# Fourteen stores moved to ScalarE's queue, a third modulation buffer, and other request points in the feed-forward sections of a two-block network

## The chip, the cores and the metric

One core of a Trainium2 chip runs the whole network for one sequence of 256 tokens. The metric is device time in microseconds from launch to end. Names of engines in views: PE is TensorE (PEld its weight loads), DVE is VectorE, ACT is ScalarE, POOL is GpSimd, SP is SyncE, which issues nearly all DMAs here.

## The reference, cut to what matters

Two blocks of two layers each run one after the other on a [256, 1024] activation, in float32. A layer of the first block is a feed-forward section, a mixer, and a second feed-forward section; each is modulated by vectors that are made from `c`:

```
mod = (silu(c) @ ada_w[l] + ada_b[l]).reshape(1, 3, 3, 1, 1024)   # 9 vectors a layer
u = modulate(h, mod[0, 0], mod[0, 1])                             # h * (1 + scale) + shift
y = (silu(u @ w_gate) * (u @ w_up)) @ w_down                      # 1024 -> 2816 -> 1024
h = layer_norm(alpha * h + 0.5 * mod[0, 2] * y, g, b)
... mixer (convolution, state-space and attention branches), layer_norm, then the same again
```

A layer of the second block is a mixer of attention and mLSTM, and a feed-forward section `x + relu(rms(x) @ w_ff1)**2 @ w_ff2` (1024 to 4096 to 1024); it has no modulation.

## The kernel before

**Weights.** Each weight is packed in halves of 128x1024 float32 (512 KB). One half is one `Unit`. `load_half` (L181) issues its DMA from SyncE into the ring `raw` (4 buffers), ScalarE copies it to `hi` in the fast float format (L187), VectorE makes the rest `lo = raw - hi` (L188), and TensorE multiplies three times, hi by hi, lo by hi, hi by lo (L284 to L286 where weights are the stationary side, L297 to L299 where they are the moving side). `run` keeps at most LIVE = 4 split units ahead of the one being multiplied.

**A feed-forward section** of the first block has 11 column chunks. Chunk j gives four units for the hidden layer (gate and up, L284 to L286), then the two `down` units of chunk j-1, so six units in a round (four in the second block). The product of gate and up, `t2d` (L808), is made on VectorE, and its split `q` on ScalarE (L701) and VectorE (L702) feeds `down`. The last four `down` units are held back and run as `row_tail`: first the upper 128 tokens, then `stats(0)`, then the lower 128 tokens. I call the sections A (layer 0, first), B (layer 0, second), C (layer 1, first), D (layer 1, second), and E and F in the second block. A has 50 units after its hand-written start, B, C and D 66.

**A boundary** (`Ln`) needs rows of gains: `fetch` loads `grow` (the gate row, through DRAM) and two `lnrow` rows, 512 KB each. `stats` (L608, L609) multiplies and adds them and takes mean and variance of each row; `nb` (L615) then lets ScalarE normalise (L619) and TensorE transpose (L432). `early` splits the first four units of the next section into spare buffers; `prefetch` ends both.

**Sides.** Work beside the units is a generator in `sides`; after each unit `step_sides` advances it by its rate. `ada_stream` makes the modulation vectors: 128 tiles of 512 KB, each loaded by SyncE (L491) into the ring `ada` and multiplied and summed on VectorE (L492). A section sets its pace with `set_pace`, whose first tile has to stay behind `src.ins`, the last instructions of the operand of that section.

**Order.** The program text gives an order; a scheduler at build time then gives each engine its own list, by what it thinks to be ready and which buffers are free. Every engine runs its list strictly from front to back, SyncE's DMA issues too: an issue that waits for its buffer holds all issues behind it.

Of the kernel before, what the change touches and what calls it, by code (L numbers as in the profile page):

```python
# [19 lines left out]
P = 128  # L20
T = 256
D = 1024
# [83 lines left out]
def net_kernel(ctx, tc, a, out, dbg=None):  # L106
# [382 lines left out]
    def ada_tile(l, j, k, col, raw):  # L489
        n = D  # L490
        nc.sync.dma_start(raw, a["adaw"][l, j, k // 2][:, (k % 2) * n:(k % 2 + 1) * n])  # L491
        V.scalar_tensor_tensor(raw, raw, 1.0, crow, op0=ALU.mult, op1=ALU.mult, accum_out=col[:, k:k + 1])  # L492
# [4 lines left out]
    def ada_stream():  # L497
        for l, j in [(l, j) for l in range(DEPTH) for j in range(9)][2:]:
            col = const.tile([P, KT], F32, name="mod%d_%d" % (l, j))
            for k in range(KT):  # L500
                with behind(pace["after"]):
                    ada_tile(l, j, k, col, rt("ada", D, 2))
                pace["after"] = ()
                yield
            V.tensor_add(col, col, adb[:, l, j * 8:j * 8 + 8])
            mods[(l, j)] = col
            if j % 3 == 2:
                yield
                tp = tp_tile()
                E.transpose(tp[0:KT, :P], col, ident)  # L510
                gr = rt("t1", T, 4)[0:KT, :P]
                S.activation(gr, tp[0:KT, :P], AF.Copy, scale=(1.0 if j == 5 else 0.5))
                nc.sync.dma_start(growd[l * 3 + j // 3].rearrange("(k p) -> k p", p=P), gr)
                mods[(l, j, "row")] = True

    def set_pace(r, after=None):
# [33 lines left out]
            late_load(rows[tt], hd[tt])  # L550
            yield

    def start_fetch(nx):

        state["fetch"] = add_side(nx.fetch(), 1.0)

    def early(nx, n=4, rate=1.0):

# [6 lines left out]
    class Ln:  # L565
# [60 lines left out]
        def residual(self, tts=(0, 1)):  # L626
            with behind(self.ins):
                for tt in tts:
                    r = self.rows[tt]
                    V.tensor_mul(r, r, self.gr[0])  # L630
                    V.tensor_add(r, r, self.gr[1])
                    S.activation(r, r, AF.Copy, scale=ALPHA)
                    if self.i == 0:
                        nc.sync.dma_start(hd[tt], r)
            if 1 in tts:
                dump("h%d%d" % (self.l, self.i), self.rows)

    class Rms:
# [30 lines left out]
        def residual(self):  # L669
            if self.src:  # L670
                for tt in range(2):
                    nc.sync.dma_start(hd[tt], self.rows[tt])

    def rms_norm(row, pre, eps, out, sq, prepare=None):

# [85 lines left out]
    def ffn(cols, down, nj, src, act, rows, nxt):  # L761

        xT = lambda: src.xT
        y, hids, items = {}, {}, []

        def hidden(j):
            st = []

            def evac(ps):
                r = act(st, ps)  # L770
                if r is not None:
                    hids[j] = split_hidden(r)
            its = []
            for c in cols(j):
                its += proj_cols(c, xT, evac)
            return its
        hold = {"nx": nxt(y)}
        n0 = NFIRST if isinstance(src, First) else 2 // len(cols(0))
        done = 0
        for j in range(n0 - 1, nj):  # L780
            if j >= n0:
                items += hidden(j)
            elif isinstance(src, First):
                first = sum((cols(i) for i in range(n0)), [])
                items.append(lambda: src.start(first, rows, hids))
                continue
            else:
                items += first_hidden(sum((cols(i) for i in range(n0)), []), xT, rows, lambda: None, hids)
            if j == n0 + 1:
                items.append(src.residual)  # L790
            items += sum(down_items(y, hids, down, nj, range(done, j), hold), [])
            done = j
            if j == nj - 3:
                items.append(lambda: start_fetch(hold["nx"]))
            if j == nj - 4:
                items.append(lambda: early(hold["nx"], 4, 1.0))
            if j == nj - 2:
                items.append(lambda: hold["nx"].prefetch())
        items += sum(down_items(y, hids, down, nj, [nj - 1], hold), [])
        return items, hold["nx"]  # L800
# [1062 lines left out]
    def ffn_section(cols, down, nj, act, rows, nxt, tiles):  # L1863
        src = cur
        items, nx = ffn(cols, down, nj, src, act, rows, nxt)
        src.pre += set_early(items)
        us = [i for i, it in enumerate(items) if isinstance(it, Unit)]
        rate = tiles / (len(us) - 7)
        if isinstance(src, First):
            items.insert(us[1], lambda: set_pace(rate, src.ins))  # L1870
            items.insert(us[1], lambda: src.finish())
        elif rate:
            items.insert(us[3], lambda: set_pace(rate, src.ins))
        return items, nx
# [41 lines left out]
    class Bridge(Rms):  # L1916
# [12 lines left out]
        def start(self):  # L1929
            self.rows = self.ln.rows  # L1930
            for tt in range(2):
# [2 lines left out]
                    self.ln.stats(1)  # L1934
                self.norm[tt] = rms_norm(self.rows[tt], 1.0, 1e-6, self.n[tt], self.n[tt], self.prepare(tt))
                self.operand(tt)
                nc.sync.dma_start(hd[tt], self.rows[tt])
                if tt == 0:
                    state["after"] = self.ins
            dump("h12", self.rows)  # L1940
# [234 lines left out]
```

## Time and profile before

| | us |
|---|---|
| median of 3 runs | 2551.43 (2548.42 to 2554.11) |
| the profiled execution, its own time | 2554.82 |
| span in its profile | 2552.7 |

The profile counts the span from the first to the last instruction of the program; 2.1 us lie around it. TensorE is the busy engine. Its matmuls overlap, so its busy time says less than its waits: a wait of TensorE names the instruction that waited and what it waited for.

### The profile page before, as it was taken

How to read it: one execution, taken by the hardware profiler on the slowest of the kernel's cores; microseconds unless marked ns; L12 is line 12 of the kernel's file. 1: busy time of each engine (PE TensorE's matmuls, PEld its weight loads, DVE VectorE, ACT ScalarE, POOL GpSimd, SP SyncE). 2: the span in 40 equal slices, each digit the busy share in tenths (PEclk: the TensorE clock that was granted, in tenths of full speed). 3: DMA queues.
4: the chain of work that ended last, by engine and by line, in shares of the span. 5: the costliest groups of instructions: out<-in, count | busy, mean ns of one | idle time of the engine just before them, and what ended most of it. 6: DMA issues, size and time to landing. Idle time of an engine off the chain costs nothing.

```text
span 2552.7 us, 42530 instructions
## 1 busy us (share of the span) xinstructions
PE 2438.5 (96%) x16604; PEld 2208.8 (87%) x16604; DVE 1839.7 (72%) x3270; ACT 1344.2 (53%) x2356; POOL 69.8 (3%) x128
## 2 busy tenths in 40 slices
PE   8999999989889989989999999999899999999999
PEld 6887889889878879978898999899789898789888
DVE  7768988899786676768988996655766555656554
ACT  5444666544543444435666546545465555555554
POOL 0000000000000000000000000000100000100000
PEclk9999999999999999989999999999999999999999
DMA  9886622256868868875522357457335456436454
GB/s 332 286 301 226 217 101 92 91 171 216 270 218 279 272 205 275 273 242 173 166 67 84 117 188 231 143 189 250 119 121 185 156 187 223 134 100 223 141 187 143
DMA packets 134218, 484.73 MB, mean 190 GB/s; under 512 B 15569, under 2 KB 16129, under 8 KB 134018
## 3 DMA queue, kind: packets, MB, share of 16 engines
q1 hardware_dynamic: 133442, 480.83, 57.0%
q8 instruction: 130, 2.13, 0.3%
q10 hardware_dynamic: 576, 1.19, 0.1%
q14 instruction: 70, 0.57, 0.1%
HBM read 476.69 MB, written 5.27 MB: 189 GB/s over the span
## 4 chain that ended last, share of the span: by engine, by line
PE 61%; DMA 15%; DVE 13%; ACT 5%; issue 4%; POOL 1%; SPq 0%; ACTq 0%; DVEq 0%; POOLq 0%
PE mm L284 10%; PE mm L285 10%; PE mm L286 10%; DMA ada<-in_adaw_dram 8%; PE y L297 6%; PE y L298 6%; PE y L299 6%; DVE lo L188 4%; DVE ca L1204 2%; PE tp L989 2%; ACT hi L187 2%; DMA raw<-in_wg_dram 2%; DVE ada L492 1%; PE tp L980 1%; DMA raw<-in_wo_dram 1%
## 5 line engine op out<-in xcount | busy, mean ns | idle before, releaser
L187 ACT ACTIVATE hi<-raw 128x1024 fp32r<-128x1024 f32 (+1 forms) x676 | 712.6, 1058 | 725.1 <-PE mm L285 367.2
L188 DVE TENSOR_TENSOR lo<-raw,hi 128x1024 fp32r<-128x1024 f32 (+1 forms) x676 | 822.2, 1221 | 304.7 <-ACT hi L187 300.9
L284 PE MATMUL mm<-xTh,hi 128*128 128x256 f32 x2896 | 827.8, 286 | 10.3 <-ACT av L1222 3.0
L286 PE MATMUL mm<-xTh,lo 128*128 128x256 f32 x2896 | 824.2, 285 | 6.5 <-DVE lo L188 6.5
L285 PE MATMUL mm<-xTl,hi 128*128 128x256 f32 x2896 | 822.5, 284 | 2.4 <-DVE xTl L455 2.4
L284 PEld LDWEIGHTS mm<-xTh,hi 128*128 128x128 f32 x2896 | 551.2, 190 | 15.9 <-ACT av L1222 3.7
L286 PEld LDWEIGHTS mm<-xTh,lo 128*128 128x128 f32 x2896 | 550.8, 190 | 9.6 <-DVE lo L188 9.0
L285 PEld LDWEIGHTS mm<-xTl,hi 128*128 128x128 f32 x2896 | 550.7, 190 | 6.5 <-DVE xTl L455 3.2
L299 PE MATMUL y<-hi,q 128*128 128x512 f32 x664 | 264.5, 399 | 1.0 <-DVE q L702 1.0
L492 DVE SCALAR_TENSOR_TENSOR ada<-ada,crow 128x1024 f32<-128x1024 f32 x128 | 156.1, 1221 | 120.7 <-DMA ada<-in_adaw_dram 120.5
L297 PE MATMUL y<-hi,q 128*128 128x512 f32 x552 | 221.8, 402 | 14.2 <-ACT q L701 14.2
L298 PE MATMUL y<-lo,q 128*128 128x512 f32 x552 | 220.7, 400 | 5.0 <-DVE lo L188 5.0
L1204 DVE SCALAR_TENSOR_TENSOR ca<-av,pcol,ca 128x244 f32<-128x244 f32 (+26 forms) x480 | 207.3, 461 | 0.3
L299 PEld LDWEIGHTS y<-hi,q 128*128 128x128 f32 x664 | 126.4, 190 | 32.4 <-DVE q L702 2.0
L297 PEld LDWEIGHTS y<-hi,q 128*128 128x128 f32 x552 | 105.3, 191 | 39.0 <-ACT q L701 16.6
L298 PEld LDWEIGHTS y<-lo,q 128*128 128x128 f32 x552 | 104.9, 190 | 29.5 <-DVE lo L188 7.5
L297 PE MATMUL y<-hi,xTh 128*128 128x512 f32 (+1 forms) x288 | 114.1, 396 | 3.1 <-DVE e8b L830 1.5
L284 PE MATMUL mm<-xyh,hi 128*128 128x256 f32 x384 | 112.2, 293 | 4.2 <-ACT t2d L1366 4.2
L285 PE MATMUL mm<-xyl,hi 128*128 128x256 f32 x384 | 111.7, 291 | 4.4 <-DVE xyl L415 4.4
L286 PE MATMUL mm<-xyh,lo 128*128 128x256 f32 x384 | 111.1, 290 | 0.8 <-DVE lo L188 0.8
L299 PE MATMUL y<-hi,xTl 128*128 128x512 f32 (+1 forms) x288 | 111.1, 386 | 0.0
L298 PE MATMUL y<-lo,xTh 128*128 128x512 f32 (+1 forms) x288 | 110.7, 384 | 0.0
(492 smaller groups left out, 3730.5 us busy)
## 6 DMA issues: line engine op xcount, KB each, us to landing
ada<-in_adaw_dram SPq DMA_DIRECT2D x128, 512.0 KB, 5.2
raw<-in_ff_dram SPq DMA_DIRECT2D x128, 512.0 KB, 4.6
raw<-in_wg_dram SPq DMA_DIRECT2D x88, 512.0 KB, 5.6
raw<-in_wu_dram SPq DMA_DIRECT2D x88, 512.0 KB, 5.6
raw<-in_wd_dram SPq DMA_DIRECT2D x88, 512.0 KB, 5.4
raw<-in_wG_dram SPq DMA_DIRECT2D x48, 512.0 KB, 4.2
raw<-in_wkv_dram SPq DMA_DIRECT2D x16, 512.0 KB, 4.6
raw<-in_wval_dram SPq DMA_DIRECT2D x16, 512.0 KB, 4.3
```

What stands on the lines that cost most here:

```text
L187: S.activation(hi, raw, AF.Copy)
L188: eng.tensor_tensor(lo, raw, f(hi), op=ALU.subtract)
L284: E.matmul(ps, wh[:, wk + k], xh, start=(k == 0), stop=False)
L285: E.matmul(ps, wh[:, wk + k], xl, start=False, stop=False)
L286: E.matmul(ps, wl[:, wk + k], xh, start=False, stop=(k == nk - 1))
L297: return [E.matmul(ps, xh, wh[:, kk, cs], start=first, stop=False), E.matmul(ps, xh, wl[:, kk, cs], start=False, stop=False), E.matmul(ps, ...
L298: E.matmul(ps, xh, wl[:, kk, cs], start=False, stop=False),
L299: E.matmul(ps, xl, wh[:, kk, cs], start=False, stop=last)]
L492: V.scalar_tensor_tensor(raw, raw, 1.0, crow, op0=ALU.mult, op1=ALU.mult, accum_out=col[:, k:k + 1])
L980: E.transpose(tp[:, tsl(r * nbr + b)], pr[:, r, b, tsl(kt)], ident)
L989: E.matmul(o[:, i * HD:(i + 1) * HD], pTs[kt][:, tsl(i)], vof(i % nbr, kt), start=(kt == 0), stop=(kt == tt))
L1204: V.scalar_tensor_tensor(ca[:, k, s:T], av[:, 0:T - s], caw[:, k, w:w + 1], ca[:, k, s:T], op0=ALU.mult, op1=ALU.add)
```

## The change

Four things change. The ring `ada` gets a third buffer. Fourteen stores that depend on computed rows (eight of `hd`, six of `growd`) are issued by ScalarE in place of SyncE. In feed-forward sections `fetch` is asked for 32 units' worth of rounds ahead of the last chunk at 0.2 steps a unit (before: two chunks ahead, one step a unit), `early` 24 units ahead at 0.25 (before: three chunks ahead, one a unit), and `prefetch` after the last hidden chunk (before: one chunk sooner). The pace of `ada_stream` in a feed-forward section goes from 26/(units - 7) to 26/(units - 18) steps a unit: 0.60 to 0.81 in A, 0.44 to 0.54 in B, C and D.

```
--- before.py
+++ after.py
@@ ada_stream
                 with behind(pace["after"]):
-                    ada_tile(l, j, k, col, rt("ada", D, 2))
+                    ada_tile(l, j, k, col, rt("ada", D, 3))
                 pace["after"] = ()
...
                 S.activation(gr, tp[0:KT, :P], AF.Copy, scale=(1.0 if j == 5 else 0.5))
-                nc.sync.dma_start(growd[l * 3 + j // 3].rearrange("(k p) -> k p", p=P), gr)
+                S.dma_start(growd[l * 3 + j // 3].rearrange("(k p) -> k p", p=P), gr)
@@ start_fetch
-    def start_fetch(nx):
+    def start_fetch(nx, rate=1.0):
 
-        state["fetch"] = add_side(nx.fetch(), 1.0)
+        state["fetch"] = add_side(nx.fetch(), rate)
@@ Ln.residual
                     S.activation(r, r, AF.Copy, scale=ALPHA)
                     if self.i == 0:
-                        nc.sync.dma_start(hd[tt], r)
+                        S.dma_start(hd[tt], r)
@@ Rms.residual
                 for tt in range(2):
-                    nc.sync.dma_start(hd[tt], self.rows[tt])
+                    S.dma_start(hd[tt], self.rows[tt])
@@ ffn
             done = j
-            if j == nj - 3:
-                items.append(lambda: start_fetch(hold["nx"]))
-            if j == nj - 4:
-                items.append(lambda: early(hold["nx"], 4, 1.0))
-            if j == nj - 2:
+            per = 2 * len(cols(0)) + 2
+            if j == nj - 1 - 32 // per:
+                items.append(lambda: start_fetch(hold["nx"], 0.2))
+            if j == nj - 1 - 24 // per:
+                items.append(lambda: early(hold["nx"], 4, 0.25))
+            if j == nj - 1:
                 items.append(lambda: hold["nx"].prefetch())
@@ ffn_section
-        rate = tiles / (len(us) - 7)
+        rate = tiles / (len(us) - 18)
@@ Bridge.start
                 self.operand(tt)
-                nc.sync.dma_start(hd[tt], self.rows[tt])
+                S.dma_start(hd[tt], self.rows[tt])
```

What the scheduler makes of it is seen in the lists of the engines. Numbers in names are buffers of one tile each; the `mod` name says which vector the product goes to.

**The first tile of a pace.** SyncE's list in the middle of section B, before, from the load of the tile whose product must stay behind C's operand (`ada_9902`):

```order
L491 DMA ada_9902<-in_adaw_dram 128x1024
L181 DMA raw_8531<-in_wu_dram 128x1024
L491 DMA ada_9968<-in_adaw_dram 128x1024
L181 DMA raw_8552<-in_wu_dram 128x1024
L181 DMA raw_8583<-in_wd_dram 128x1024
L491 DMA ada_10043<-in_adaw_dram 128x1024
L181 DMA raw_8618<-in_wd_dram 128x1024
L181 DMA raw_8649<-in_wg_dram 128x1024
```

VectorE's list at the start of C, before, where that tile is used:

```order
L188 TENSOR_TENSOR lo_9759<-raw_9756,hi_9758 128x1024
L455 TENSOR_TENSOR xTl_9669<-t2_9732,xTh_9668 128x2x128
L455 TENSOR_TENSOR xTl_9669<-t2_9737,xTh_9668 128x2x128
L814 TENSOR_TENSOR t2d_9811<-t2d_9811,mm_9762 128x256
L492 SCALAR_TENSOR_TENSOR ada_9902,mod1_2_9294<-ada_9902,crow_95 128x1024
L759 TENSOR_TENSOR q4_9814<-tp_9815,q4_9814 128x2x128
L505 TENSOR_TENSOR mod1_2_9294<-mod1_2_9294,adb_86 128x8
```

18 products of other tiles stand between that load and this use, so the tile keeps one of the two `ada` buffers from the middle of B to the start of C.

SyncE's list in section B with the change, from the load of the corresponding tile (`ada_9871`):

```order
L491 DMA ada_9871<-in_adaw_dram 128x1024
L181 DMA raw_8592<-in_wu_dram 128x1024
L491 DMA ada_9988<-in_adaw_dram 128x1024
L181 DMA raw_8623<-in_wd_dram 128x1024
L491 DMA ada_10056<-in_adaw_dram 128x1024
L181 DMA raw_8658<-in_wd_dram 128x1024
L491 DMA ada_10097<-in_adaw_dram 128x1024
L181 DMA raw_8689<-in_wg_dram 128x1024
```

VectorE's list at the start of C with the change, where it is used:

```order
L815 TENSOR_TENSOR t2d_9862<-t2d_9862,mm_9813 128x256
L455 TENSOR_TENSOR xTl_9720<-t2_9783,xTh_9719 128x2x128
L455 TENSOR_TENSOR xTl_9720<-t2_9788,xTh_9719 128x2x128
L492 SCALAR_TENSOR_TENSOR ada_9871,mod1_4_9488<-ada_9871,crow_95 128x1024
L759 TENSOR_TENSOR q4_9865<-tp_9866,q4_9865 128x2x128
L505 TENSOR_TENSOR mod1_4_9488<-mod1_4_9488,adb_86 128x8
```

The tile is kept over the end of B as before, now as one of three buffers, and its load stands later (the 93rd tile in SyncE's list, before the 79th).

**End of C.** VectorE's list before, from the next to last `k` split to the first boundary row (`t2d` is the last hidden product, `q` its split, `y` the first row product of the boundary):

```order
L702 TENSOR_TENSOR q_11419<-t2d,q_11419 128x512
L188 TENSOR_TENSOR lo<-raw,hi 128x1024
L188 TENSOR_TENSOR k_11470<-raw,zc 128x1024
L492 SCALAR_TENSOR_TENSOR ada,mod_8_16208<-ada,crow 128x1024
L188 TENSOR_TENSOR lo<-raw,hi 128x1024 x2
L492 SCALAR_TENSOR_TENSOR ada,mod_8_16208<-ada,crow 128x1024
L188 TENSOR_TENSOR lo<-raw,hi 128x1024 x2
L492 SCALAR_TENSOR_TENSOR ada,mod_8_16208<-ada,crow 128x1024
L808 TENSOR_TENSOR t2d<-t2d,mm 128x512
L188 TENSOR_TENSOR lo<-raw,hi 128x1024
L702 TENSOR_TENSOR q_11595<-t2d,q_11595 128x512
```

The same place with the change:

```order
L702 TENSOR_TENSOR q_11480<-t2d,q_11480 128x512
L188 TENSOR_TENSOR lo<-raw,hi 128x1024
L188 TENSOR_TENSOR k_11539<-raw,zc 128x1024
L188 TENSOR_TENSOR lo<-raw,hi 128x1024 x4
L809 TENSOR_TENSOR t2d<-t2d,mm 128x512
L188 TENSOR_TENSOR lo<-raw,hi 128x1024
L702 TENSOR_TENSOR q_11666<-t2d,q_11666 128x512
```

The three `ada` products are gone from this place; the splits `lo` stay. In SyncE's list the last of all 128 `ada` loads stands ahead of C's `grow` row now; before, six of them stood behind it.

**End of B.** VectorE's list before, from the first row product of the boundary to `nb`:

```order
L608 TENSOR_TENSOR y_7991<-y_7991,grow 128x512
L608 TENSOR_TENSOR row_7219<-row_7219,y_7991 128x512
L609 BN_STATS bnst<-row_7219 128x6
L492 SCALAR_TENSOR_TENSOR ada,mod_4_10704<-ada,crow 128x1024
L608 TENSOR_TENSOR y_7991<-y_7991,grow 128x512
L608 TENSOR_TENSOR row_7219<-row_7219,y_7991 128x512
L609 BN_STATS bnst<-row_7219 128x6
L465 BN_AGGR bnmv<-bnst 128x2
L460 TENSOR_SCALAR rstd<-bnmv 128x1
L615 SCALAR_TENSOR_TENSOR nb<-bnmv,rstd 128x1
```

The same place with the change:

```order
L608 TENSOR_TENSOR y_8025<-y_8025,grow 128x512
L492 SCALAR_TENSOR_TENSOR ada,mod_7_11142<-ada,crow 128x1024
L608 TENSOR_TENSOR row_7250<-row_7250,y_8025 128x512
L609 BN_STATS bnst<-row_7250 128x6
L608 TENSOR_TENSOR y_8025<-y_8025,grow 128x512
L492 SCALAR_TENSOR_TENSOR ada,mod_7_11142<-ada,crow 128x1024
L608 TENSOR_TENSOR row_7250<-row_7250,y_8025 128x512
L492 SCALAR_TENSOR_TENSOR ada,mod_7_11142<-ada,crow 128x1024
L609 BN_STATS bnst<-row_7250 128x6
L465 BN_AGGR bnmv<-bnst 128x2
L460 TENSOR_SCALAR rstd<-bnmv 128x1
L615 SCALAR_TENSOR_TENSOR nb<-bnmv,rstd 128x1
```

One `ada` product stood between the first row product and `nb`; three stand there now.

In numbers over SyncE's list: the `ada` loads ahead of the next section's first `wval` load are 34 in A (before 26), and 24 units from A's `grow` row to the last `down` load are accompanied by 18 `ada` loads, 4 early units and 3 rows (in the last 24 units before: 10, 4 and 3).

## Rows read from the trace of the kernel before

**Rows 1.** The page, part 1: busy us, share, instructions.

```profile
PE 2438.5 (96%) x16604; PEld 2208.8 (87%) x16604; DVE 1839.7 (72%) x3270; ACT 1344.2 (53%) x2356; POOL 69.8 (3%) x128
```

**Rows 2.** Windows: length, then busy us (instructions) PE, PEld, DVE, ACT, POOL; clock; DMA.

```profile
73.00:221.00 148.00, 139.93 (x897) 125.72 (x897) 103.10 (x136) 58.56 (x65) 0.55 (x1) 0.99 0.84 290
720.00:934.00 214.00, 198.44 (x1343) 180.11 (x1341) 151.14 (x207) 93.04 (x120) 1.12 (x2) 0.98 0.77 257
934.00:1143.00 209.00, 197.64 (x1337) 181.99 (x1337) 146.65 (x202) 89.72 (x113) 1.14 (x2) 0.97 0.76 255
1608.00:1804.00 196.00, 191.40 (x1337) 178.22 (x1337) 116.74 (x134) 91.95 (x118) 2.00 (x3) 0.99 0.57 189
```

**Rows 3.** Waits in section A (73:221): total us, times, longest.

```profile
DVE ada L492 <- DMA ada<-in_adaw_dram: 25.0, 19, 2.7
...
PE y L297 <- ACT q L701: 3.3, 1, 3.3
```

**Rows 4.** Waits in section B (720:934).

```profile
DVE ada L492 <- DMA ada<-in_adaw_dram: 44.9, 25, 4.1
...
PE y L297 <- ACT q L701: 4.6, 1, 4.6
...
PE mm L286 <- DVE lo L188: 3.0, 5, 1.1
...
PE y L298 <- DVE lo L188: 2.6, 4, 1.1
```

**Rows 5.** Waits in section C (934:1143).

```profile
DVE ada L492 <- DMA ada<-in_adaw_dram: 43.9, 22, 3.7
...
PE y L297 <- ACT q L701: 5.3, 1, 5.3
...
PE mm L284 <- ACT hi L187: 1.9, 1, 1.9
```

**Rows 6.** Waits in section D (1608:1804).

```profile
PE tp L432 <- ACT t L452: 1.2, 1, 1.2
```

**Rows 7.** Windows at the ends of B and C (columns as in Rows 2).

```profile
917.20:927.40 10.20, 8.29 (x19) 6.03 (x20) 6.33 (x10) 0.63 (x1) 0.00 (x0) 0.50 0.64 224
1091.30:1098.00 6.70, 6.09 (x28) 6.09 (x29) 5.88 (x7) 4.06 (x5) 0.00 (x0) 0.50 0.78 244
1128.80:1135.60 6.80, 5.05 (x12) 3.99 (x13) 3.57 (x7) 0.63 (x1) 0.00 (x0) 0.50 0.66 244
```

**Rows 8.** VectorE in order of time, end of C (1114:1131.5).

```profile
1123.00 1.23 DVE L492 SCALAR_TENSOR_TENSOR ada<-ada,crow 128x1024 f32<-128x1024 f32 x1 [3.69 <-DMA ada<-in_adaw_dram]
...
1129.15 0.68 DVE L808 TENSOR_TENSOR t2d<-t2d,mm 128x512 f32<-128x512 f32 x1
```

**Rows 9.** VectorE in order of time, middle of B (800:815).

```profile
807.66 1.23 DVE L492 SCALAR_TENSOR_TENSOR ada<-ada,crow 128x1024 f32<-128x1024 f32 x1 [3.43 <-DMA ada<-in_adaw_dram]
```

**Rows 10.** SyncE in order of time, middle of B (800:815).

```profile
808.92 0.33 SPq L491 DMA_DIRECT2D ada<-in_adaw_dram  x1
```

**Rows 11.** Windows: the first 50 us, and the last 69 us of A.

```profile
0.00:50.00 50.00, 38.38 (x146) 29.08 (x147) 36.94 (x60) 22.60 (x27) 0.20 (x4) 1.00 0.96 359
142.00:211.00 69.00, 60.93 (x418) 55.36 (x418) 49.78 (x60) 31.48 (x34) 0.00 (x0) 1.00 0.88 302
```

**Rows 12.** DMA issues: KB each, median us to landing.

```profile
raw<-in_wg_dram SPq DMA_DIRECT2D x88, 512.0 KB, 5.6
...
t<-in_lnrow_dram SPq DMA_DIRECT2D x12, 512.0 KB, 8.3
```

**Rows 13.** SyncE's own waits, whole span.

```profile
SPq L491 <- DVE ada L492: 230.1, 81, 7.9
...
SPq L634 <- ACT row L632: 16.9, 4, 5.1
```

**Rows 14.** The page, part 5: split of a weight half on ScalarE and VectorE (busy, mean ns).

```profile
L187 ACT ACTIVATE hi<-raw 128x1024 fp32r<-128x1024 f32 (+1 forms) x676 | 712.6, 1058 | 725.1 <-PE mm L285 367.2
L188 DVE TENSOR_TENSOR lo<-raw,hi 128x1024 fp32r<-128x1024 f32 (+1 forms) x676 | 822.2, 1221 | 304.7 <-ACT hi L187 300.9
```

## The prediction

> **What bounds the kernel now.** I began with the page's first part: TensorE is busy for 96% of the span [rows 1], so time can only be won where it stands still or runs at a lower clock. The second view was windows by section. B, C and D have the same 66 units and nearly the same TensorE instructions (1343, 1337, 1337), yet take 214, 209 and 196 us [rows 2]. D is the yardstick: it fetches rows and early units at the same points as B and C, but has no `ada` stream; its DMA share is 0.57 against 0.77 and 0.76, its clock 0.99 against 0.98 and 0.97. So B holds 18 us and C 13 us that D doesn't have. D's 196/66 = 2.97 us is the price of a unit, and A's 148/50 = 2.96 us says that A holds almost nothing to win.
>
> The third view was waits by section, to see what fills those 18 and 13 us. In B TensorE waits 4.6 us in one piece for `q`, and 3.0 and 2.6 us in nine short ones for `lo` [rows 4]; in C 5.3 us for `q` and 1.9 us for `hi` [rows 5]; D's largest wait is 1.2 us and there is none for `q` [rows 6]. To that comes a lower clock: three stretches at 0.50, which is 1.2 of 2.4 GHz, 10.2 us at B's end and 6.7 and 6.8 us at C's [rows 7]. In the stretches at the ends TensorE had stood in those waits or in the boundary just before. At half clock the same matmuls take twice as long, so such a stretch costs at most half its length.
>
> The fourth view says why `q` is late. VectorE works its list from front to back, and in it `ada` products wait for their own loads: 44.9 us in B, 43.9 us in C, 25.0 us in A [rows 3 to 5]. At C's end one product starts at 1123.00 after 3.69 us of such a wait, and the last hidden product `t2d`, from which `q` is split, only runs at 1129.15 [rows 8]. The loads are late because only one of the two `ada` buffers turns round: the other one keeps the first tile of the next pace, which must stay behind the next operand. In the middle of B the product ends at 807.66 + 1.23 = 808.89 [rows 9], and SyncE issues the next load at 808.92 [rows 10]. Over the span SyncE was held so 81 times, 230.1 us in all, 2.84 us each [rows 13].
>
> **The change, part by part.** The sum is made against the profiled execution, 2554.82 us; this is 3.4 us above the median of 2551.43, so 3.4 comes off at the end.
>
> *Third buffer and higher pace, section C.* Two buffers turn round, and the stream has ended ahead of C's `grow` row. The three products in front of the last `t2d` are gone, and with them the waits that `q` stood behind. To win: 5.3 + 1.9 us of waits and half of 6.7 + 6.8 us, 13.9 us in all. The boundary of a section without `ada` still shows D's 1.2 us, and some of the low clock may be due to the boundary itself, so I take 11. Two products of 1.23 us also leave the row chain of the boundary, where TensorE stands still: 2.4 more, as they are ahead of `nb` there. Together **-13**, which is also C's whole distance from D. Bounds: -4 if only one of waits and clock goes partly, -17 if everything goes.
>
> *Section B.* To win: 4.6 + 3.0 + 2.6 us of waits and half of 10.2 us, 15.3 us. The tile for C's operand is still parked, but two buffers are left, not one; `ada` products go on to B's end, so I take two thirds, -10. Against it, three products stand in the row chain ahead of `nb`, before one: 2 x 1.23 = +2.4. Sum **-8**. Bounds: -15, and +5 if the waits stay and the chain's products have to wait for a load as that of 807.66 did (3.43 us).
>
> *Section A.* Here 8 more `ada` tiles than before fall in the section. From the `grow` row on, 24 units go with 18 `ada` loads, 4 early units and 3 rows: 49 loads of 512 KB, 25.7 MB. The time for 24 units is 24 x 2.97 = 71.3 us, so 360 GB/s are asked for. The last 69 us of A gave 302 GB/s at a DMA share of 0.88 [rows 11], which is 343 GB/s if it were full: 74.9 us, 3.6 us short. The four live units can hide some of that, and A's 3.3 us for `q` may go or stay; I take **+3**. Bounds: 25.7 MB at the 302 GB/s as delivered are 85 us, +14; if the shortage is hidden and the `q` wait goes, -3. VectorE has room: 49.78 of 69 us busy now, 8 more products of 1.23 us make it 59.6 us, 86%. A rule of the Trainium skill bears on this term ("DMA: Bandwidth & Descriptors", section "Bandwidth", Where 436 GB/s comes from): between HBM and SBUF the memory's side limits a core to about 358 GB/s. By it the 25.7 MB take an estimated 71.8 us, the live units hide the rest, the term would be 0 and the sum 3 us lower. The first 50 us of this trace show 359 GB/s at a share of 0.96, which agrees with that figure; the stretch in A doesn't reach it.
>
> *`fetch`, `early`, `prefetch` at other points.* The same 3 rows and 4 units are loaded, spread over more units. No wait for a row stands among the waits of A to D, and a row lands 8.3 us after its issue, under three units [rows 12]. In D, E and F this is the only part of the change besides stores; D has 1.2 us to give. I take **-1** for the three together (0 to -2). `prefetch` moves by one chunk, and what it waits for was landed long before. The early splits are the same work, 1.06 us on ScalarE and 1.22 us on VectorE for a unit [rows 14].
>
> *Fourteen stores by ScalarE.* SyncE was held 16.9 us in four waits for the rows that it stored [rows 13], with weight loads behind them. No wait for weights of that size shows in TensorE, since units are loaded ahead, so nothing is won that isn't counted above. On ScalarE an issue costs about the 0.33 us of SyncE's [rows 10], 14 x 0.33 = 4.6 us on an engine that is busy for 53% [rows 1]. Behind such a store stand the copies `hi`. Its operand is ScalarE's own result, so it hardly waits. Bounds -3 and +3, I take **0**.
>
> *Mixers.* They get a few more or fewer `ada` products; TensorE's list there is the same work. **0**, bounds -3 and +3.
>
> Sum: -13 - 8 + 3 - 1 = -19, so 2554.8 - 19 = 2535.8 for the profiled execution, and less 3.4 about **2532** for the median.
>
> **Rivals.** *Slower, by a held SyncE queue.* A load whose buffer is not free holds the weight loads behind it. A's last third gets 8 more `ada` loads; if each is held 2.84 us as they are now, that is 22.7 us, and four live units cover 4 x 2.97 = 11.9 us: A +11. If B's end goes the same way, it is +11 there with 2.4 in its chain, and C and D give back 14: +10, about **2562**. It decides from 11.9/8 = 1.5 us of holding for each added load. For it speaks the DMA share of 0.88 in A already [rows 11]; against it that the third buffer is there so that the wait falls, and that A now loses little with 25.0 us of waits in VectorE [rows 3]. *No change: the work is only moved.* All 128 tiles have to be loaded beside weights anyway. If A's end delivers 302 GB/s as now, A pays +14 for what C gives, -13, while in B waits go and the longer chain and a low clock stay, about 0: about **2551**. *More than forecast.* B and C both fall to D's length, -18 and -13, and A pays nothing: with -1 this is -32, about **2519**. For it speaks that the same 1337 instructions ran in 196 us; against it that B keeps its stream to the end.
>
> **How the numbers follow.** Forecast 0.57, no change 0.18, slower 0.15, more than forecast 0.10. Times within 0.2%, about 5 us, can't be told from no change here. Faster is the forecast and the larger gain, 0.67; the same 0.18; slower 0.15. The forecast's own range, with the bounds of B and C not both at one end, is 2520 to 2545. The range that holds 8 in 10 reaches down past the larger gain, to 2514, and up over the case of no change, to 2556; what is left out is the slower rival and a little below.
>
> **What would show it.** C near 198 us, with a clock of 1.00 at its end, no `q` wait above 2 us there, and no `ada` product after its `grow` row. VectorE's waits for `ada` loads well below 44.9 us in B. B near 206 us; its end without the wait for `q`, but the chain from the first row product to `nb` some 2 us longer. A near 151 us with a DMA share above 0.9 in its last third. SyncE's waits at the stores gone. I am wrong if TensorE waits for `hi` or `lo` in A or B for more than 10 us (the feed falls short), if an `ada` product in a row chain waits for its load, or if a mixer is longer by more than 3 us.

## The result, and the profile after

The changed kernel takes 2530.77 us (median of 4 runs, 2530.0 to 2533.14), the kernel before 2551.78 us beside it. The ratio on record is 0.9914, with a 95% interval of 0.9897 to 0.9931 (the two medians alone give 0.9918). The forecast was 2532 us. The profiled execution took 2530.0 us, with a span of 2528.1 us; TensorE's share of the span is as before [rows 1]:

```profile
PE 2428.6 (96%) x16604; PEld 2202.1 (87%) x16604; DVE 1839.9 (73%) x3270; ACT 1344.3 (53%) x2356; POOL 69.8 (3%) x128
```

The sum came out near the forecast, but not its terms. Windows of both kernels, cut at the second `nb` of each boundary (before, then after; the rows are the first section, the mixer of layer 0, B, C, the mixer of layer 1, and all the rest; columns as in rows 2):

```profile
0.00:228.80 228.80, 206.94 (x1192) 178.12 (x1193) 166.93 (x242) 105.37 (x137) 1.42 (x6) 0.99 0.84 295
228.80:725.70 496.90, 466.16 (x3325) 425.98 (x3325) 427.31 (x916) 279.88 (x578) 19.29 (x40) 0.97 0.51 169
725.70:939.70 214.00, 199.17 (x1350) 180.90 (x1349) 151.37 (x206) 93.04 (x119) 1.14 (x2) 0.98 0.77 257
939.70:1150.80 211.10, 199.36 (x1335) 183.08 (x1333) 148.13 (x202) 90.86 (x117) 1.09 (x2) 0.96 0.75 252
1150.80:1611.10 460.30, 450.42 (x3321) 413.57 (x3320) 393.05 (x853) 278.02 (x576) 20.60 (x41) 1.00 0.45 147
1611.10:2552.70 941.60, 916.45 (x6092) 827.19 (x6091) 552.90 (x854) 496.98 (x834) 26.23 (x38) 0.99 0.52 167
```

```profile
0.00:218.70 218.70, 203.60 (x1188) 176.28 (x1189) 174.26 (x254) 104.73 (x138) 1.59 (x6) 1.00 0.91 327
218.70:710.30 491.60, 460.95 (x3326) 421.16 (x3325) 431.29 (x928) 280.63 (x579) 19.57 (x40) 0.98 0.53 176
710.30:929.00 218.70, 201.66 (x1351) 184.16 (x1350) 163.65 (x228) 95.34 (x121) 2.03 (x2) 0.95 0.80 276
929.00:1122.10 193.10, 190.81 (x1329) 176.92 (x1328) 123.98 (x156) 89.05 (x115) 1.10 (x2) 0.99 0.65 213
1122.10:1588.50 466.40, 456.83 (x3332) 418.88 (x3331) 394.60 (x852) 279.26 (x577) 19.05 (x40) 0.99 0.45 145
1588.50:2528.10 939.60, 914.75 (x6088) 824.70 (x6086) 552.12 (x854) 495.32 (x834) 26.41 (x38) 0.99 0.52 168
```

| | forecast | before | after | difference | TensorE idle, before and after | half clock, before and after |
|---|---|---|---|---|---|---|
| start and A | +3 | 228.8 | 218.7 | -10.1 | 21.9, 15.1 | 3.4, 0.0 |
| mixer of layer 0 | 0 | 496.9 | 491.6 | -5.3 | 30.7, 30.6 | 34.1, 20.3 |
| B | -8 | 214.0 | 218.7 | +4.7 | 14.8, 17.0 | 10.2, 20.7 |
| C | -13 | 211.1 | 193.1 | -18.0 | 11.7, 2.3 | 17.1, 2.0 |
| mixer of layer 1 | 0 | 460.3 | 466.4 | +6.1 | 9.9, 9.6 | 1.0, 8.3 |
| D and block 2 | -1 | 941.6 | 939.6 | -2.0 | 25.2, 24.9 | 13.2, 12.0 |
| sum | -19 | 2552.7 | 2528.1 | -24.6 | 114.2, 99.5 | 79.0, 63.3 |

"Idle" is a section's length less the busy time of PE in the lines above; "half clock" is the time in the section at a granted clock of 0.50 (in A recorded from about 24 us on). If half clock costs at most half its length, the two columns account for up to 22.6 of the 24.6 us: 14.7 of idle time and up to 7.9 of clock.

C did what was expected, and more of it: VectorE's waits for `ada` loads fell from 43.9 us [rows 5] to 6.7 us with only 11 of the 128 tiles left for it (before: 32), and the largest wait of TensorE is the boundary's own (waits from 929 to 1122 us):

```profile
DVE ada L492 <- DMA ada<-in_adaw_dram: 6.7, 6, 2.2
...
PE tp L432 <- ACT t L452: 1.2, 1, 1.2
```

B did not. Its waits are those of before, some larger [rows 4] (710 to 929 us):

```profile
DVE ada L492 <- DMA ada<-in_adaw_dram: 40.5, 26, 4.8
...
PE y L297 <- ACT q L701: 6.6, 1, 6.6
```

VectorE in order of time at B's end shows why. Before the change an `ada` product that waits 3.18 us for its load stands two splits ahead of the last hidden product `t2d`:

```profile
913.24 1.23 DVE L492 SCALAR_TENSOR_TENSOR ada<-ada,crow 128x1024 f32<-128x1024 f32 x1 [3.18 <-DMA ada<-in_adaw_dram]
...
916.66 0.68 DVE L808 TENSOR_TENSOR t2d<-t2d,mm 128x512 f32<-128x512 f32 x1
```

With the change one stands right ahead of `t2d`, and it waits 3.38 us. Behind it `q` is late. In the row chain, from the first `y` product (910.32) to `nb` (919.26), stand the three `ada` products that the list announced:

```profile
903.52 1.23 DVE L492 SCALAR_TENSOR_TENSOR ada<-ada,crow 128x1024 f32<-128x1024 f32 x1 [3.38 <-DMA ada<-in_adaw_dram]
...
904.67 0.68 DVE L809 TENSOR_TENSOR t2d<-t2d,mm 128x512 f32<-128x512 f32 x1
...
906.41 0.69 DVE L702 TENSOR_TENSOR q<-t2d,q 128x512 fp32r<-128x512 f32 x1
...
910.32 0.70 DVE L608 TENSOR_TENSOR y<-y,grow 128x512 f32<-128x512 f32 x1 [3.14 <-PE y L299]
910.92 1.22 DVE L492 SCALAR_TENSOR_TENSOR ada<-ada,crow 128x1024 f32<-128x1024 f32 x1
...
914.51 1.22 DVE L492 SCALAR_TENSOR_TENSOR ada<-ada,crow 128x1024 f32<-128x1024 f32 x1
...
916.25 1.22 DVE L492 SCALAR_TENSOR_TENSOR ada<-ada,crow 128x1024 f32<-128x1024 f32 x1
...
919.26 0.16 DVE L615 SCALAR_TENSOR_TENSOR nb<-bnmv,rstd 128x1 f32<-128x1 f32 x1 [0.75 <-POOL rstd L461]
```

TensorE stood still until 906.1 us in that 6.6 us wait for `q`. Its granted clock was 0.50 for 10.1 us around the wait's end, and for 6.7 us more after the row chain; at B's end before it was 0.50 for 10.2 us [rows 7]:

```profile
901.70:911.80 10.10, 5.73 (x14) 4.47 (x15) 5.13 (x8) 0.63 (x1) 0.00 (x0) 0.50 0.75 286
922.20:928.90 6.70, 5.32 (x24) 4.59 (x23) 6.31 (x13) 6.33 (x13) 1.39 (x1) 0.50 0.47 153
```

A is the surprise. The same stretch at A's end, before and after:

```profile
133.00:202.00 69.00, 64.24 (x446) 58.93 (x445) 48.48 (x57) 31.00 (x33) 0.00 (x0) 1.00 0.87 297
```

```profile
133.00:202.00 69.00, 68.89 (x484) 64.18 (x483) 60.24 (x78) 34.19 (x39) 0.00 (x0) 1.00 0.99 367
```

It shows 78 instructions of VectorE in place of 57, 367 GB/s in place of 297, and TensorE idle for 0.1 us in place of 4.8.

### The profile page after: what moved, and what is told of

Read it like the earlier page. It is cut to its first block, busy times and chain, and to the rows that moved or that the text cites. A ratio compares the mean times of both kernels' runs of the same rounds, so it can differ in the third digit from the quotient of the medians.

```text
span 2528.1 us, 42522 instructions
## 1 busy us (share of the span) xinstructions
PE 2428.6 (96%) x16604; PEld 2202.1 (87%) x16604; DVE 1839.9 (73%) x3270; ACT 1344.3 (53%) x2356; POOL 69.8 (3%) x128
## 4 chain that ended last, share of the span: by engine, by line
PE 68%; DVE 13%; DMA 10%; ACT 4%; issue 4%; POOL 0%; SPq 0%; ACTq 0%; DVEq 0%; POOLq 0%
PE mm L284 11%; PE mm L285 11%; PE mm L286 11%; PE y L297 7%; PE y L298 7%; PE y L299 7%; DVE lo L188 5%; DMA ada<-in_adaw_dram 5%; DVE ca L1205 3%; PE tp L990 2%; ACT hi L187 1%; DMA raw<-in_wg_dram 1%; DMA raw<-in_wo_dram 1%; PE tp L981 1%; DVE ada L492 1%
## 5 line engine op out<-in xcount | busy, mean ns | idle before, releaser
L297 PE MATMUL y<-hi,q 128*128 128x512 f32 x552 | 219.8, 399 | 6.8 <-ACT q L701 6.8
L1205 DVE SCALAR_TENSOR_TENSOR ca<-av,pcol,ca 128x244 f32<-128x244 f32 (+23 forms) x480 | 206.8, 458 | 0.4
L297 PEld LDWEIGHTS y<-hi,q 128*128 128x128 f32 x552 | 104.3, 189 | 30.6 <-ACT q L701 8.7
```

The costliest lines, as they stand in the source:

```text
L297: return [E.matmul(ps, xh, wh[:, kk, cs], start=first, stop=False), E.matmul(ps, xh, wl[:, kk, cs], start=False, stop=False), E.matmul(ps, ...
L1205: V.scalar_tensor_tensor(ca[:, k, s:T], av[:, 0:T - s], caw[:, k, w:w + 1], ca[:, k, s:T], op0=ALU.mult, op1=ALU.add)
```

## The experiments

Sections are cut at the second `nb` of each boundary as above, from one profiled execution each; times are medians, the ratio is to the kernel before on the same chip.

| run | time, us | ratio (95%) | A | mixer 0 | B | C | mixer 1 |
|---|---|---|---|---|---|---|---|
| before | | 1 | 228.8 | 496.9 | 214.0 | 211.1 | 460.3 |
| the change | 2530.8 | 0.9914 (0.9897 to 0.9931) | 218.7 | 491.6 | 218.7 | 193.1 | 466.4 |
| 1 third buffer alone | 2530.2 | 0.9917 (0.9898 to 0.9936) | 228.9 | 487.4 | 209.4 | 195.9 | 461.4 |
| 2 pace alone | 2543.3 | 0.9970 (0.9956 to 0.9983) | 230.5 | 499.0 | 214.6 | 193.8 | 462.4 |
| 3 stores alone | 2551.9 | 0.9991 (0.9977 to 1.0004) | 227.1 | 494.5 | 211.8 | 212.0 | 461.1 |
| 4 request points alone | 2555.5 | 1.0021 (1.0007 to 1.0036) | 228.1 | 494.1 | 213.0 | 209.6 | 462.0 |
| 5 before, none parked | 2545.5 | 0.9962 (0.9949 to 0.9975) | 232.0 | 490.5 | 217.8 | 197.3 | 463.4 |
| 6 change without buffer | 2552.9 | 0.9993 (0.9981 to 1.0005) | 232.6 | 496.6 | 219.8 | 196.9 | 464.7 |
| 7 change without points | 2534.6 | 0.9925 (0.9910 to 0.9940) | 219.7 | 491.3 | 217.5 | 192.6 | 464.0 |
| 8 all tiles behind | 2524.0 | 0.9884 (0.9869 to 0.9898) | 218.8 | 487.2 | 204.8 | 204.5 | 465.3 |
| 9 the same, two buffers | 2541.7 | 0.9935 (0.9912 to 0.9957) | 226.6 | 487.6 | 210.5 | 201.0 | 466.2 |
| 10 fewer in B and C | 2518.1 | 0.9852 (0.9830 to 0.9873) | 215.9 | 486.5 | 200.2 | 197.4 | 472.8 |
| 11 fewer in the mixer | 2518.2 | 0.9851 (0.9831 to 0.9870) | 217.2 | 478.4 | 204.8 | 197.4 | 475.6 |
| 12 mixer emptied | 2517.1 | 0.9847 (0.9825 to 0.9869) | 219.3 | 472.1 | 211.1 | 201.0 | 463.2 |

A section of one profiled execution is good to a few us: the last 940 us, which hold nothing of the stream but seven tiles in runs 10 and 11, differ by up to 8 us between runs (939.6 to 947.5).

**The parts alone (1 to 4).** Two theories stood against each other: that the buffer carries the gain, or that the pace does.

```
@@ 1, on the kernel before
-                    ada_tile(l, j, k, col, rt("ada", D, 2))
+                    ada_tile(l, j, k, col, rt("ada", D, 3))
@@ 2, on the kernel before
-        rate = tiles / (len(us) - 7)
+        rate = tiles / (len(us) - 18)
@@ 3, on the kernel before (and the same for hd, three times)
-                nc.sync.dma_start(growd[l * 3 + j // 3].rearrange("(k p) -> k p", p=P), gr)
+                S.dma_start(growd[l * 3 + j // 3].rearrange("(k p) -> k p", p=P), gr)
@@ 4, on the kernel before (and start_fetch with its rate, as in the change's diff)
-            if j == nj - 3:
-                items.append(lambda: start_fetch(hold["nx"]))
-            if j == nj - 4:
-                items.append(lambda: early(hold["nx"], 4, 1.0))
-            if j == nj - 2:
+            per = 2 * len(cols(0)) + 2
+            if j == nj - 1 - 32 // per:
+                items.append(lambda: start_fetch(hold["nx"], 0.2))
+            if j == nj - 1 - 24 // per:
+                items.append(lambda: early(hold["nx"], 4, 0.25))
+            if j == nj - 1:
...
```

> The kernel before with only the third ada buffer. In VectorE's list no ada product is left behind C's grow row, the last t2d of B has three splits between itself and the nearest ada product, and the chain of A holds two of them. Theory 1 (the parked tile left one buffer to turn, so the third buffer carries the gain): C about -17 us, B about -8, A about -3, in all 2520 to 2532 us. Theory 2 (the pace carries it, because it moves seven more tiles into A and so fewer are left for C): the buffer alone gives less than half of the 21 us, 2541 to 2550 us.

> The kernel before with only the higher pace. A takes seven more tiles (50 before its boundary, as with the whole change), and C's end is free of ada products, with two buffers of which one is still parked in B and C. Theory 1: VectorE still waits some 3.5 us for a load in each product in B, so B stays at its length; C gets its end free, -10 us; A pays up to 3: 2540 to 2546 us. Theory 2: all of A's and C's gain is here, -9 and -17 us: 2522 to 2530 us.

> The kernel before with only the fourteen stores moved to ScalarE. Both theories: no change, 2548 to 2554 us. A third one, that SyncE's 16.9 us of waits at the stores hold weight loads that TensorE needs, would give 2540 us or less.

> The kernel before with only the request points of fetch, early and prefetch moved. In C one ada product still stands right ahead of the last t2d, and none in the row chain. Theory 1: the row chain of C is 2.4 us shorter, the rest stays, 2546 to 2552 us. Theory 2: the same. If the spreading of the early loads is what takes the waits for lo away in A and B, 2535 to 2542 us.

The third buffer alone gives the whole gain, 0.9917 against 0.9914, so theory 1 holds for the total. It does not hold for all of the places. In the profile of run 1 C gives 15.2 us and B 4.6, A nothing, and the mixer of layer 0 gives 9.5 us with the same 31 tiles, which no theory named. Pace alone is worth 0.3%, some 8 us: in its profile C gives 17, and every other section takes a little. The stores can't be told from nothing, and the request points alone cost 0.2%, a little outside of what either theory allowed.

Over the whole span, what the buffer changes is how long SyncE is held at `ada` loads, 230.1 us in 81 cases before [rows 13]. The lines are of the changed kernel, of the buffer alone and of the pace alone:

```profile
SPq L491 <- DVE ada L492: 128.0, 45, 8.7
```

```profile
SPq L491 <- DVE ada L492: 127.8, 50, 7.7
```

```profile
SPq L491 <- DVE ada L492: 247.1, 80, 11.1
```

With the buffer alone B is 209.4 us. Two splits lie between the last `ada` product and `t2d` there, as before the change, but the product's wait is 1.85 us in place of 3.18, and TensorE waits 1.3 us for `q`. One product in the row chain then waits 3.12 us for its load (VectorE, end of B in that run):

```profile
900.44 1.23 DVE L492 SCALAR_TENSOR_TENSOR ada<-ada,crow 128x1024 f32<-128x1024 f32 x1 [1.85 <-DMA ada<-in_adaw_dram]
...
901.59 2.36 DVE L188 TENSOR_TENSOR lo<-raw,hi 128x1024 fp32r<-128x1024 f32 x2
903.86 0.68 DVE L808 TENSOR_TENSOR t2d<-t2d,mm 128x512 f32<-128x512 f32 x1
...
905.59 0.69 DVE L702 TENSOR_TENSOR q<-t2d,q 128x512 fp32r<-128x512 f32 x1
...
912.46 1.23 DVE L492 SCALAR_TENSOR_TENSOR ada<-ada,crow 128x1024 f32<-128x1024 f32 x1 [3.12 <-DMA ada<-in_adaw_dram]
```

A gains nothing from the buffer alone and nothing from the pace alone, for two reasons. With the buffer alone the stream reaches A's row chain: one product right ahead of the chain waits 4.08 us for its load, two more stand in the chain, and TensorE waits 4.9 us for the normalised row (VectorE, then the waits of that run from 133 to 229 us). With both, no product stands between the first row product (204.9 us in the changed kernel) and `nb` (211.2).

```profile
211.38 1.23 DVE L492 SCALAR_TENSOR_TENSOR ada<-ada,crow 128x1024 f32<-128x1024 f32 x1 [4.08 <-DMA ada<-in_adaw_dram]
```

```profile
PE tp L432 <- ACT row L619: 5.8, 2, 4.9
```

With the pace alone SyncE is held, and the weights come late. These are SyncE's waits at `ada` loads from 73 to 219 us, and VectorE's waits for the same loads, with the pace alone:

```profile
SPq L491 <- DVE ada L492: 47.0, 22, 5.5
```

```profile
DVE ada L492 <- DMA ada<-in_adaw_dram: 17.3, 13, 2.9
...
PE y L297 <- ACT hi L187: 4.6, 3, 3.3
```

The same in the changed kernel:

```profile
SPq L491 <- DVE ada L492: 16.8, 8, 7.1
```

```profile
DVE ada L492 <- DMA ada<-in_adaw_dram: 16.2, 14, 2.6
```

An `ada` load that finds no free buffer holds the weight loads behind it, 47.0 us in 22 cases; with three buffers it is 16.8 us in 8. TensorE's waits for `hi` and `lo` in this window are 8.1 us in run 2, and none stands among its waits in the changed kernel. VectorE's own waits for the ring hardly differ, 17.3 and 16.2 us: they don't show the harm. At A's end run 2 moves 330 GB/s where the changed kernel moves 367:

```profile
133.00:202.00 69.00, 64.29 (x446) 58.42 (x444) 54.75 (x72) 30.23 (x34) 0.00 (x0) 1.00 0.93 330
```

**Is it the parked tile? (5, 6, 7).** If the tile parked over the boundary is the fault, then two buffers of which none is parked should do nearly as well as three.

```
@@ 5, on the kernel before
-                with behind(pace["after"]):
+                if True:
@@ 6, on the changed kernel
-                    ada_tile(l, j, k, col, rt("ada", D, 3))
+                    ada_tile(l, j, k, col, rt("ada", D, 2))
@@ 7, on the changed kernel: the edit of run 4 taken back
```

> The kernel before with two ada buffers, but the first tile of a pace no longer has to stay behind the section's operand, so none is parked. C's list is free of ada products before its end; four products stand in B's row chain ahead of nb, before one. Theory 1 (two turning buffers are enough; the parked tile was the fault): VectorE's waits for ada loads fall below 35 us in B, C about -16 us, B 0 to -5, in all 2528 to 2540 us. Rival (a third load on its way is what is needed, parked or not): waits stay above 40 us in B, and at most 8 us are won, 2545 us or more.

> The whole change with two buffers again. Theory 1: about as with the pace alone, 2538 to 2548 us, VectorE's waits in B above 40 us, A at 228 to 231 us. If the 10 us that the whole change wins in A come from pace and request points together, without the buffer: A about 219 us and 2530 to 2537 us.

> The whole change with the request points of before. If A's 10 us come from pace and buffer together: A about 219 us, in all 2525 to 2533 us. If the spread early units are needed for them: A 228 us or more, 2535 to 2542 us.

Run 5 comes out nearer the rival. Its 2545.5 us and its waits are what the rival allowed, though 9.8 us are won against its 8. The gain is not in B, where VectorE still waits 40.7 us for its loads although both buffers turn (722 to 940 us):

```profile
DVE ada L492 <- DMA ada<-in_adaw_dram: 40.7, 27, 5.1
```

But its list also puts more products into B's row chain, so it doesn't part the two theories cleanly; run 9 does it better, below. Run 6 missed my range: without the buffer, pace, stores and request points together win nothing, and A, at 232.6 us, is the longest of all. Run 7 is as expected for A: it is 219.7 us, so its 10 us come from buffer and pace together, and the request points are not needed for them. Its total, 2534.6 us, is 1.6 us above the range that I gave; its ratio lies within the interval of the changed kernel.

**The end of the section (8, 9).** B's loss in the changed kernel was put down to the products at its end. Keeping every tile of a pace behind the operand of its own section (one line less) stops the stream from running into B's end, and parks nothing.

```
@@ 8, on the changed kernel
                 with behind(pace["after"]):
                     ada_tile(l, j, k, col, rt("ada", D, 3))
-                pace["after"] = ()
                 yield
@@ 9, on run 8
-                    ada_tile(l, j, k, col, rt("ada", D, 3))
+                    ada_tile(l, j, k, col, rt("ada", D, 2))
```

> The whole change, and every tile of a pace, not only its first, stays behind the section's operand, so that no tile is parked and none runs ahead of its section. The lists have no ada product in the last six splits and in the row chain of B and of C, nor at the end of the mixer of layer 0; C has 31 products in place of 11, the mixer of layer 1 six. Theory 1 with B's end as its gap (products ahead of the last t2d and of nb): B falls from 219 to about 203 us, C stays within 4 us of 193, 2508 to 2522 us. Rival (the products cost their time wherever they stand): what B wins, C and the mixer of layer 1 lose, 2526 to 2536 us.

> The kernel with all tiles behind their section's operand, with two ada buffers in place of three; nothing is parked, the numbers of tiles by section are the same (A 50, mixer 26, B 31, C 31, mixer 6), and the ends of B and C are as free of products. Theory 1 as first put (a parked tile is the fault, two turning buffers are enough): within 5 us of three buffers, 2520 to 2530 us. Theory 1 amended (a load takes 5 to 8 us, so two buffers still leave VectorE waiting for it and three are needed): A back at 228 to 232 us, B and C 4 to 8 us longer each, 2538 to 2550 us.

Run 8 is faster than the changed kernel, 0.9884 against 0.9914, with intervals that just touch. B falls to 204.8 us as expected; TensorE's waits for `q` at its end are 1.4 us at most. C goes to 204.5 us, which I had not expected: it now holds 31 tiles in place of 11. The total lies between the two theories. The free end is not all of B's gain, since B holds 14 tiles fewer, and no run parts the two. At the price that C paid for its 20 more, 11.4/20 = 0.57 us, they are worth 8 of the 13.9 us, which leaves 6 for the end; at the price of C's 39 tiles in run 12, 7.9/28 = 0.28 us, it is 4 and 10. Run 9 has the same number of tiles in every section and nothing parked, and is 0.5% slower than run 8, in the range of the amended theory: three buffers are needed for themselves, and the parked tile is only a part of what was wrong before. The order inside the sections differs a little between the two lists. It is A and B that pay, 7.8 and 5.7 us; C doesn't. SyncE's own waits in A, 73 to 219 us, with three buffers and with two:

```profile
SPq L491 <- DVE ada L492: 8.4, 5, 4.5
```

```profile
SPq L491 <- DVE ada L492: 42.0, 21, 5.5
```

**Where the tiles should stand (10, 11, 12).** All three are run 8 with other rates, set by section. The number in the call is the 26 of the pace, so a lower one means fewer steps a unit.

```
-                its, nx = mixer_section(mixer1, l, nxt, 26.0)
...
-                                      swiglu_rows, nxt, 26.0)
@@ 10, on run 8
+                its, nx = mixer_section(mixer1, l, nxt, (26.0, 6.0)[l])
...
+                                      swiglu_rows, nxt, ((26.0, 22.0), (22.0, 8.0))[l][n])
@@ 11, on run 8
+                its, nx = mixer_section(mixer1, l, nxt, (16.0, 6.0)[l])
...
+                                      swiglu_rows, nxt, ((26.0, 22.0), (24.0, 8.0))[l][n])
@@ 12, on run 8
+                its, nx = mixer_section(mixer1, l, nxt, (8.0, 0.0)[l])
...
+                                      swiglu_rows, nxt, ((30.0, 34.0), (34.0, 8.0))[l][n])
```

> All tiles behind, three buffers, and lower rates in B and C, so that these hold 26 tiles each in place of 31, the mixer of layer 1 holds 9 in place of 6, and D the last 7. If tiles above some 25 in a section cost about 0.5 us each and D takes its seven for nothing: B and C 2 to 3 us shorter each, the mixer of layer 1 up to 3 longer, 2516 to 2523 us. If the number of tiles in a section doesn't matter once its end is free: 2522 to 2527 us.

> As the run with lower rates in B and C, but the mixer of layer 0 holds 17 tiles in place of 26 and that of layer 1 eleven in place of 9. The mixer of layer 0 is 22 us longer than that of layer 1 with 26 tiles more; if that is the price of the tiles, 0.8 us each, it falls by 7 us and the total by 3 to 7. If the 22 us are something else in layer 0: the total stays within 3 us of the other run.

> All tiles behind, three buffers; the mixer of layer 0 is left with 9 tiles, A takes 56, B 40, C 39, the mixer of layer 1 none. If a tile costs 0.8 us in the mixer and 0.5 us in B and C: mixer -14 us, B and C +4 to +5 each, A +3, mixer of layer 1 -4: 2515 to 2522 us. If the feed-forward sections are short of transfers with 40 tiles (40 + 66 + 7 loads of 512 KB in some 200 us are 296 GB/s, under the 367 GB/s that A's end delivered): they lose 10 us or more each, 2526 to 2540 us.

All three take 2517 to 2518 us, 1.5% less than the kernel before. That is 0.3% less than run 8, with intervals that just touch its own. The three can't be told apart, and the sections say why: the mixer of layer 0 takes 486.5, 478.4 and 472.1 us with 26, 17 and 9 tiles, which is 0.85 us a tile; but the tiles that leave it cost about as much where they go. The mixer of layer 1 takes 472.8 us with 9 and 463.2 us with none. In B and C the price of a tile is not clear from single executions: B takes 200.2 us (run 10) and 204.8 us (run 11) with 26 tiles, 204.8 with 31 (run 8) and 211.1 with 40; C takes 204.5 us with 31 and 201.0 with 39. Run 11 thus found the price that it looked for (8.1 us in that mixer) and no gain. Its list puts 17 tiles in the mixer of layer 1, where the expectation says eleven, and that mixer is the longest of all. In run 10 that mixer is 7.5 us longer than in run 8, where up to 3 were expected. In run 12 C became shorter, by 3.5 us, where 4 to 5 longer was expected.

## Why the prediction was right, and where it was not

**The total** was right, 2530.8 us against 2532, and so was the part of the change that carries it, third buffer and pace. The prediction didn't separate the two; runs 1, 2 and 6 do, and it is the buffer. That the sum came out was luck in part: A was 13 us better than its term, B 13 us worse, and the two cancelled. Both mixers and A lie outside the bounds given for them, and C 1 us outside. One of its own signs of being wrong came, a mixer longer by more than 3 us (6.1 in these two executions); two signs of being right did not, VectorE's waits in B well below 44.9 us and B near 206 us.

**C** (-13, measured -18.0): the mechanism was right. The `q` and `hi` waits are gone, half clock fell from 17.1 to 2.0 us, and the row chain is free of `ada`. The term was undersized: idle time fell by 9.4 us and the clock gave up to 7.5, so the bound of -17 was nearer. The pace alone does this too (run 2: 193.8 us with 22 tiles in place of 32), and so does nearly the buffer alone (195.9 us with 23).

**B** (-8, measured +4.7): this step failed. I argued that two turning buffers would take away two thirds of the waits. VectorE's waits for loads only went from 44.9 to 40.5 us, while the stream took more tiles through B (45 in place of 35 between the marks), and an `ada` product ahead of the last `t2d` kept its wait and stood nearer to it. Where the product stands two splits ahead and waits less (run 1) B is 209.4 us with 42 tiles; where no product stands at the end (run 8) it is 204.8 us with 31. The three products in the chain were foreseen, 2.4 us; from its first row product to `nb` the chain grew by 1.1 us, from 7.9 to 8.9. That a second stretch at half clock would follow it was not foreseen.

**A** (+3, measured -10.1): this step failed twice. I took 343 GB/s for what the transfers can give, by scaling 302 GB/s at a share of 0.88 [rows 11] up to 1. The changed kernel moved 367 GB/s at 0.99 there, more than the 360 that I said were asked for. It is also more than the about 358 GB/s of the Trainium skill ("DMA: Bandwidth & Descriptors", section "Bandwidth", Where 436 GB/s comes from), which that page gives as half of what two cores share, and this program runs on one; the measurement decides, but the term by that rule, 0, was nearer than mine. The 302 GB/s were what was asked for there, not what the transfers could give: 41 loads went with those 24 units before, 49 now, and 41 loads of 512 KB in the 71.3 us of 24 units are 301 GB/s. And I took A to hold almost nothing, because a unit took 2.96 us in it as in D. That count was wrong. The window from 73 to 221 us holds the matmuls of 48 units, not of 50 (210 at line 284 with 8 for a hidden unit, 88 at line 297 with 4 for a `down` unit), 3.07 us each, and TensorE was idle for 8.1 of its 148 us, against 4.6 of D's 196 [rows 2]. In the changed kernel the same matmuls take from 73 to 211 us, 2.86 us a unit, with 0.4 us of idle time.

**The slower rival**, a held SyncE queue, was the right mechanism in the wrong kernel: it is what the pace does without the buffer (47.0 us of holding in A in run 2, 42.0 in run 9). With the third buffer it is 16.8 us, so the rival's time didn't come in the changed kernel.

**Stores, request points**: taken as 0 and -1; runs 3 and 4 show 0.9991 and 1.0021 alone. SyncE's waits at line 634 [rows 13] are gone from the list of its waits, and run 3 shows no time that they had cost. Run 7 leaves out the points and keeps A's gain.

**Mixers**: taken as 0. That of layer 0 won 5.3 us, with 36 tiles in place of 31 between the marks. TensorE's idle time there is the same but for 0.1 us, so in these two executions the gain is one of clock, at most 6.9 us. With the buffer alone it won 9.5 (idle 24.2 us, half clock 23.9). That of layer 1 lost 6.1 us. It holds one tile of the stream in both kernels, TensorE is idle in it no longer than before and has no wait above 2 us; half clock explains at most 3.6 us (8.3 in place of 1.0 us of it). The runs with one tile or none there lie from 460.3 to 466.4 us, in no order that I could tie to an edit. Why the clock falls more or less often in the mixers, and what the buffer alone wins in the first, stays open.

## What to carry to other kernels

A ring whose load waits for its buffer on a shared issue queue stops every load behind it. The waits of the engine that uses the ring don't show that (17.3 and 16.2 us in A, with SyncE held 47.0 and 16.8 us); look at the waits of the issuing queue. Here a further buffer was worth 0.8%, and a higher pace without it little (0.3% alone, nothing together with stores and request points). Work beside a tight chain should be kept out of the last stretch of the section by its place in the order (run 8); the higher rate did that in C and not in B, where one product ahead of the last dependent operation cost its own wait and a stretch at half clock. A rate that was asked for, scaled up by its busy share, was too low a limit here (343 GB/s, against 367 moved); 359 GB/s at a share of 0.96 in the same trace [rows 11] was the better guess. A price per unit needs the units counted in the window that is timed.

## What the runs showed of the hardware

- A sustained 367 GB/s at a share of 0.99 over 69 us, with TensorE busy for 68.89 of them, on one core. The rate for a full share was not constant over the stretches read: 302/0.88 = 343, 359/0.96 = 374 [rows 11], 367/0.99 = 371 GB/s.
- A product of 1.23 us on VectorE cost the mixer of layer 0 about 0.85 us of its length, although VectorE is busy for 421.28 of 486.50 us there (run 10, window of the mixer) and the products there wait for their loads only once, 1.3 us. Of the 14.4 us between 26 and 9 tiles, 10.5 are idle time of TensorE (24.0 and 13.5 us in runs 10 and 12).
